# Undivided probabilities and transposed weights as the stationary operand in a decoder layer's prompt attentions

## The chip, the cores and the metric

The kernel runs on one core of a Trainium2 chip. The metric is the device time of one execution in microseconds. Three runs of the kernel before gave 4417.42, 4426.75 and 4428.59 us; the median is 4426.75 us. One more execution was profiled, and every row below is from that one.

Five engines run side by side, each strictly in the order of its own instruction list: TensorE (PE, whose weight loads are listed apart as PEld), VectorE (DVE), ScalarE (ACT), GpSimd (POOL) and SyncE (SP, which only starts transfers).

## The reference, cut to what matters

One layer of a hybrid decoder is computed for a prompt of 1024 tokens and for 64 sample tokens. Two of its parts are touched here, for the prompt only: the FoX attention (8 heads of 64, causal, with a forgetting term added to the scores) and the attention over 256 memory tokens (4 heads of 128). Both end in the same two steps, a softmax and a product with the values:

```python
# FoX, block by block of 128 queries
s = einsum('bqhd,bkhd->bhqk', qi, k) * scale + (di - dk)
s = where(k_pos <= pi, s, -inf)
p = softmax(s, axis=-1)
o = einsum('bhqk,bkhd->bqhd', p, v)
# memory
p = softmax(einsum('bthd,bmhd->bhtm', q, mk) * MEM_HD ** -0.5, axis=-1)
o = einsum('bhtm,bmhd->bthd', p, mv)
```

The division of the softmax is by one sum for each query and head, so it can be made on the probabilities or on the output. Around this lie a gated linear attention (GLA), three output projections with gates, and PEER: each token picks 128 of 16384 experts and sums what they give.

## The kernel before, in words

The tokens are cut into nine blocks: prompt blocks 0 to 7 of 128 tokens, and the sample block. `base(grp)` takes three groups in turn: [0, 1, 2], [3, 4, 5] and [sample, 6, 7]. For a group it runs all projections, GLA, FoX, memory attention, gates, output projection and the scores of PEER. Queries and heads are worked in two halves: half 0 has FoX heads 0 to 3 and memory heads 0 and 1, half 1 the others. So `fox_prompt` and `mem_prompt_att` are each called 16 times, once for a block and half.

The experts of blocks 0, 1, 2, 6 and 7 are gathered row by row (`peer_gather`): POOL starts an indirect transfer of 512 KB (L1040 for u, L1051 for v), and DVE works on the 128 x 1024 tile that landed (L1042 for u, L1057 for v). That is 256 such tiles for a block, with four buffers. Blocks 0 to 2 are gathered beside the base work of groups 1 and 2; blocks 6 and 7 beside the dense stage. The other four blocks go through `peer_dense`, which multiplies all experts on PE and ends the kernel.

The order is set by the tile framework: it takes the instructions in program order, moves the gather to a later priority, and lets a simulated timeline choose for each engine which ready instruction comes next. [...]

In `fox_prompt` the keys come in chunks of up to 512 columns: one chunk for blocks 0 to 3, two for blocks 4 to 7. For each head PE makes the scores in a PSUM bank `f` (two banks, L562, L563, L566), DVE takes the negated row maximum (L567, and L570 where there are two chunks), ACT makes the exponentials and their row sum (L575), DVE adds the sums (L578) and inverts (L579), ACT multiplies the probabilities by that (L581), PE transposes them into a bank `g` (two banks, L584), ACT copies them out (`PT`, by the helper `evac`, L99), and PE multiplies them with the values into `po` (one bank, L589). There the value columns of a head (64) are the stationary operand and the transposed probabilities (128 columns) the moving one, so `po` holds the output transposed: head dimension on the partitions. One copy (L99, `oT<-po`) ends the call, and SP writes `oT` to memory (L659). `mem_prompt_att` does the same for two heads at once (L598, L601, L604, L605, L607, L610, L99, L616).

float32 matmuls stand in the trace as two records each (L589: 576 records for 288 matmuls); a transpose is one record.

## Time and profile before

| | us |
|---|---|
| median of three runs | 4426.75 |
| the profiled execution, as a whole | 4433.77 |
| its span, first to last instruction | 4432.0 |
| base work of group 0, no gather beside it | 0 to some 710 |
| base work of groups 1 and 2, gather of blocks 0 to 2 beside it | some 710 to 2690 |
| end of group 2, start of the dense stage | 2690 to some 3100 |
| dense stage | 3108 to 4432 |

The FoX calls stand at 235 to 278 and 360 to 403 us (group 0, half 0 and half 1), 938 to 1029 and 1152 to 1244 us (group 1), 1968 to 2048 and 2214 to 2303 us (group 2). The memory calls stand at 400 to 436, 1249 to 1285 and some 2608 to 2632 us.

A table of stretches lists for each engine the busy time in it and, in brackets, the number of instructions, then the granted TensorE clock (PEclk, share of full speed), the busy share of the DMA engines and what they moved. A group of instructions has its busy time, the mean of one in ns, and the idle time of its engine just before them with what ended it.

### The profile page before, as it was taken

To read this page: it belongs to the slowest core of one execution; us is meant where nothing else is said; L and a number is where in the kernel's file an instruction comes from. 1 tells how busy PE (TensorE), PEld (TensorE's weight loads), DVE (VectorE), ACT (ScalarE), POOL (GpSimd) and SP (SyncE) were. 2 spreads that over 40 slices of the span, in tenths; PEclk is the share of its full clock that TensorE was granted. 3 is DMA by queue.
4 is the path that set the end of the run, shared out by engine and by line. 5 is a ranking of instruction groups with operands and counts; after the bars stand their busy time and mean duration, and the time that the engine had idled before them with its cause. 6 is when DMAs were issued, how large, how long until landed. Compare 5 with 4: busy or idle time off the path is not lost. (4 is left out here: it accounts for less than half of the span.)

```text
span 4432.0 us, 62344 instructions
## 1 busy us (share of the span) xinstructions
PE 3755.6 (85%) x21306; PEld 3288.8 (74%) x21306; DVE 3346.1 (75%) x7924; ACT 1796.2 (41%) x3637; POOL 1679.1 (38%) x1466
## 2 busy tenths in 40 slices
PE   4998998676689775787679979986999999999998
PEld 4886997564378775575556558875999899999997
DVE  3443469988788898888885457578999888888883
ACT  2555444343343333465564334444333223323332
POOL 0000003545644444534455553003445454545530
PEclk8997998787689886677689989997999999999999
DMA  3322457888899987778788899548999999999982
GB/s 110 90 84 70 131 165 227 279 274 294 277 309 332 319 267 242 260 243 273 253 277 287 307 321 320 169 140 289 329 303 339 327 332 337 341 337 327 344 297 81
DMA packets 652340, 1141.32 MB, mean 258 GB/s; under 512 B 62158, under 2 KB 445798, under 8 KB 648439
## 3 DMA queue, kind: packets, MB, share of 16 engines
q0 software_dynamic: 193616, 704.99, 45.6%
q1 hardware_dynamic: 458406, 432.35, 30.3%
q8 instruction: 169, 2.77, 0.2%
q14 instruction: 149, 1.21, 0.1%
HBM read 1073.45 MB, written 63.74 MB: 257 GB/s over the span
## 5 line engine op out<-in xcount | busy, mean ns | idle before, releaser
L1040 POOL DMA_INDIRECT u<-in_peer_u_dram,ei x640 | 783.3, 1224 | 873.2 <-DVE a L1042 347.6
L1051 POOL DMA_INDIRECT v<-in_peer_v_dram,ei x640 | 762.3, 1191 | 865.0 <-DVE acc L1057 452.6
L1042 DVE CUSTOM_DVE_ANT_0 u<-u,x 128x1024 f32<-128x1024 f32 x640 | 774.2, 1219 | 129.9 <-DMA u<-in_peer_u_dram,ei 128.3
L1057 DVE SCALAR_TENSOR_TENSOR acc<-v,a,acc 128x1024 f32<-128x1024 f32 x635 | 811.6, 1278 | 70.6 <-DMA v<-in_peer_v_dram,ei 68.2
L265 ACT ACTIVATE wh<-wr 128x512 fp32r<-128x512 f32 x568 | 354.0, 630 | 595.0 <-PE pj L274 186.2
L267 DVE TENSOR_TENSOR wl<-wr,wh 128x512 fp32r<-128x512 f32 x568 | 386.6, 685 | 219.4 <-PE pj L277 63.8
L1210 PE MATMUL py<-dwh,dvh 128*128 128x448 f32 x1024 | 373.9, 370 | 31.3 <-ACT dwh L1197 28.6
L1187 PE MATMUL pa<-xh,duh 128*128 128x448 f32 x1024 | 384.8, 376 | 1.3 <-ACT duh L1168 1.3
L1188 PE MATMUL pa<-xl,duh 128*128 128x448 f32 x1024 | 379.0, 370 | 0.0
L273 PE MATMUL pj<-aT,wh 128*128 128x384 f32 (+1 forms) x1104 | 367.3, 337 | 11.4 <-ACT X L837 4.5
L1211 PE MATMUL py<-dwl,dvh 128*128 128x448 f32 x1024 | 375.4, 367 | 1.4 <-DVE dwl L1198 1.4
L1212 PE MATMUL py<-dwh,dvl 128*128 128x448 f32 x1024 | 373.4, 368 | 0.3 <-DVE dvl L1206 0.3
L274 PE MATMUL pj<-aT,wh 128*128 128x384 f32 (+1 forms) x1104 | 362.3, 332 | 1.7 <-DVE aT L317 1.7
L281 PE MATMUL pj<-wh,aT 128*128 128x256 f32 x944 | 262.1, 301 | 30.3 <-DVE z L720 10.9
L1205 ACT ACTIVATE dvh<-dvr 128x1024 fp32r<-128x1024 f32 x128 | 134.2, 1059 | 377.2 <-PE py L1211 206.6
L282 PE MATMUL pj<-wh,aT 128*128 128x256 f32 x944 | 258.8, 297 | 2.9 <-DVE aT L847 1.5
L277 PE MATMUL pj<-aT,wl 128*128 128x384 f32 (+1 forms) x1104 | 251.8, 335 | 10.3 <-DVE wl L267 10.1
L1117 PE MATMUL cw<-hot,hot 128*128 128x128 f32 x768 | 173.9, 363 | 92.7 <-ACT stg L1118 73.8
L1190 PE MATMUL pa<-xh,dul 128*128 128x448 f32 x1024 | 240.2, 369 | 0.0
L1117 PEld LDWEIGHTS cw<-hot,hot 128*128 128x128 f32 x768 | 134.8, 248 | 138.1 <-ACT stg L1118 103.3
L1210 PEld LDWEIGHTS py<-dwh,dvh 128*128 128x128 f32 x1024 | 192.4, 189 | 48.6 <-ACT dwh L1197 28.9
L273 PEld LDWEIGHTS pj<-aT,wh 128*128 128x128 f32 x1104 | 213.1, 193 | 17.4 <-ACT X L837 6.6
(475 smaller groups left out, 8439.3 us busy)
## 6 DMA issues: line engine op xcount, KB each, us to landing
wr<-in_w_in_dram SPq DMA_DIRECT2D x168, 512.0 KB, 4.8
dvr<-in_peer_v_dram SPq DMA_DIRECT2D x128, 512.0 KB, 7.5
dur<-in_peer_u_dram SPq DMA_DIRECT2D x128, 512.0 KB, 6.6
dc<-c_scr SPq DMA_DIRECT2D x15, 1792.0 KB, 17.4
wr<-in_w_pq_dram SPq DMA_DIRECT2D x48, 512.0 KB, 4.3
c_scr<-stg SPq DMA_DIRECT2D x24, 1024.0 KB, 6.9
wr<-in_w_out_dram SPq DMA_DIRECT2D x24, 512.0 KB, 4.8
u<-in_peer_u_dram,ei POOLq DMA_INDIRECT x640, 6.2
```

Of the source, the lines that this page charges most:

```text
L267: V.tensor_tensor(wl, raw[:, q2:q2 + 2], wh.bitcast(F32), op=OP.subtract)
L273: PE.matmul(ps, wh[:, i, c], hi[:, k], start=k == 0, stop=False)
L274: PE.matmul(ps, wh[:, i, c], lo[:, k], start=False, stop=False)
L1040: G.indirect_dma_start(out=r, out_offset=None, in_=UR, in_offset=bass.IndirectOffsetOnAxis(ap=ei[:, s:s + 1], axis=0))
L1042: V.tensor_tensor_reduce(r, r, x2, 1.0, 0.0, OP.mult, OP.add, a[:, s:s + 1])
L1051: G.indirect_dma_start(out=r, out_offset=None, in_=VR, in_offset=bass.IndirectOffsetOnAxis(ap=ei[:, s:s + 1], axis=0))
L1057: V.scalar_tensor_tensor(acc, r, a[:, s:s + 1], acc, op0=OP.mult, op1=OP.add)
L1187: PE.matmul(pa[:, :NT], uh[:, k], xh[:, k], start=k == 0, stop=False)
L1188: PE.matmul(pa[:, :NT], uh[:, k], xl[:, k], start=False, stop=False)
L1210: PE.matmul(py[:, :NT], vh[:, j], wh, start=j == 0, stop=False)
L1211: PE.matmul(py[:, :NT], vh[:, j], wl, start=False, stop=False)
L1212: PE.matmul(py[:, :NT], vl[:, j], wh, start=False, stop=j == DG - 1)
```

## The change

The multiplication of the probabilities by the inverted sum (L581, L607) is taken out. The transposed probabilities become the stationary operand and the values the moving one, so `po` holds the output with the queries on the partitions, the four heads of a half side by side. There, once in a call, DVE adds the sums of all four heads, inverts them, and multiplies `po` by them into a tile `o` (from the pool `ge`, three buffers). Two PE transposes into a `g` bank and a copy then give `oT` as before.

```diff
         po = PS("po")
+        l = T("sm", [128, 8])
...
-                l = T("sm", [128, 4])
...
-                    A.activation(pm[:, :n], ps[ci][:, :n], AF.Exp, bias=nm[:, 0:1], accum_out=l[:, ci:ci + 1])
...
-                if len(chunks) == 2:
-                    V.tensor_tensor(l[:, 0:1], l[:, 0:1], l[:, 1:2], op=OP.add)
-                V.reciprocal(l[:, 2:3], l[:, 0:1])
...
-                    A.activation(Pm[ci][:, :n], Pm[ci][:, :n], AF.Copy, scale=l[:, 2:3])
...
+                A.activation(pm[:, :n], ps[ci][:, :n], AF.Exp, bias=nm[:, 0:1], accum_out=l[:, 4 * ci + hh:4 * ci + hh + 1])
...
-                        PE.matmul(po[64 * e:64 * e + 64, j * 128:(j + 1) * 128],
-                                  vv[:, kb, (2 * j + e) * 64:(2 * j + e + 1) * 64],
-                                  pts[:, i * 128:(i + 1) * 128], start=kb == 0, stop=kb == blk)
-        evac(oT, po[:, :256].rearrange("p (j t) -> p j t", t=128))
+                    PE.matmul(po[:, hh * 64:(hh + 1) * 64], pts[:, i * 128:(i + 1) * 128],
+                              vv[:, kb, hh * 64:(hh + 1) * 64], start=kb == 0, stop=kb == blk)
+        if nc_ == 2:
+            V.tensor_tensor(l[:, 0:4], l[:, 0:4], l[:, 4:8], op=OP.add)
+        V.reciprocal(l[:, 0:4], l[:, 0:4])
+        o = T("ge", [128, 256])
+        V.tensor_tensor(o.rearrange("p (h d) -> p h d", h=4), po[:, :256].rearrange("p (h d) -> p h d", h=4),
+                        l[:, 0:4, None].to_broadcast([128, 4, 64]), op=OP.mult)
+        pt = PS("g")
         for j in range(2):
+            PE.transpose(pt[:, j * 128:(j + 1) * 128], o[:, j * 128:(j + 1) * 128], ident)
+        evac(oT, pt[:, :256].rearrange("p (j t) -> p j t", t=128))
```

`mem_prompt_att` is changed in the same way (L607 goes, the operands of L616 change places, and a multiplication, two transposes and the copy follow).

Because the lists are chosen anew, all of them move a little. Below, rows of the lists are shown without times; names are tiles with their buffer numbers, and lines are those of the kernel that the list belongs to. In the changed kernel the scores are L565, L566 and L569, the maximum L570, the transposes L579, the value product L584, the multiplication L590 and the last transposes L594; the gather's u and v instructions are L1050 and L1065.

PE, group 1, half 0, from the last transposes of block 4's fourth head on; in the kernel before:

```order
L584 MATMUL g_11119<-c_76,P_11112 128x128 x4
L584 MATMUL g_11131<-c_76,P_11114 128x128
L589 MATMUL po_10991<-PT_11124,kv_10339 64x128 x4
L589 MATMUL po_10991<-PT_11133,kv_10339 64x128
L562 MATMUL f_11179<-c_270,c_196 128x512
L563 MATMUL f_11179<-kv_10338,zq_10895 128x512
L562 MATMUL f_11183<-c_270,c_196 128x256
```

The same place in the changed kernel:

```order
L569 MATMUL f_11117<-c_88,c_78 128x128
L584 MATMUL po_10974<-kv_10327,PT_11087 128x64 x4
L584 MATMUL po_10974<-kv_10327,PT_11097 128x64
L594 MATMUL g_11104<-c_76,ge_11102 128x128 x2
L579 MATMUL g_11125<-c_76,P_11123 128x128 x4
L565 MATMUL f_11146<-c_270,c_196 128x512
L566 MATMUL f_11146<-kv_10326,zq_10883 128x512
```

The last transposes of a block (L594) now stand straight behind its last value product, and the next head's transposes and scores behind them.

DVE, the same place (the first two heads of block 5); in the kernel before:

```order
L567 TENSOR_REDUCE sm_11140<-f_11141 128x1
L567 TENSOR_REDUCE sm_11140<-f_11145 128x1
L570 TENSOR_TENSOR sm_11140<-sm_11140 128x1
L1042 ISA u_7425,a_7055<-u_7425,x_1341_7053 128x1024
L1042 ISA a_7055 128x1
L578 TENSOR_TENSOR sm_11151<-sm_11151 128x1
L579 RECIPROCAL sm_11151<-sm_11151 128x1
L1042 ISA u_7428,a_7055<-u_7428,x_1341_7053 128x1024
L1042 ISA a_7055 128x1
L567 TENSOR_REDUCE sm_11178<-f_11179 128x1
L567 TENSOR_REDUCE sm_11178<-f_11183 128x1
```

In the changed kernel (L588 inverts the sums of block 4, L590 multiplies its output):

```order
L588 RECIPROCAL sm_10975<-sm_10975 128x4
L267 TENSOR_TENSOR wl_12264<-wr_12244,wh_12262 128x512
L570 TENSOR_REDUCE sm_11112<-f_11113 128x1
L1050 ISA u_7407,a_7043<-u_7407,x_1347_7041 128x1024
L1050 ISA a_7043 128x1
L570 TENSOR_REDUCE sm_11112<-f_11117 128x1
L1050 ISA u_7410,a_7043<-u_7410,x_1347_7041 128x1024
L1050 ISA a_7043 128x1
L590 TENSOR_TENSOR ge_11102<-po_10974,sm_10975 128x256
L573 TENSOR_TENSOR sm_11112<-sm_11112 128x1
L1050 ISA u_7413,a_7043<-u_7413,x_1347_7041 128x1024
L1050 ISA a_7043 128x1
```

The adding and inverting for each head is gone from between the maxima; the multiplication stands once, behind a gather tile.

DVE, group 2, where the third output projection is gated (the two L842, L850 in the changed kernel, of its second quarter of columns); in the kernel before:

```order
L1057 SCALAR_TENSOR_TENSOR acc_8912<-v_9592,a_8809,acc_8912 128x1024
L267 TENSOR_TENSOR wl_24304<-wr_24300,wh_24302 128x512
L1016 TENSOR_TENSOR acc_8912<-acc_8912,h_9595 128x1024
L841 TENSOR_TENSOR X_24290<-f_24254,X_24290 128x320
L841 TENSOR_TENSOR X_24294<-f_24255,X_24294 128x320
L267 TENSOR_TENSOR wl_24320<-wr_24300,wh_24318 128x512
L267 TENSOR_TENSOR wl_24338<-wr_24334,wh_24336 128x512
L842 TENSOR_TENSOR z_23478<-z_23478,X_24290 128x320
L842 TENSOR_TENSOR z_23478<-z_23478,X_24294 128x320
```

In the changed kernel:

```order
L1065 SCALAR_TENSOR_TENSOR acc_8900<-v_9550,a_8797,acc_8900 128x1024
L267 TENSOR_TENSOR wl_24188<-wr_24168,wh_24186 128x512
L267 TENSOR_TENSOR wl_24216<-wr_24212,wh_24214 128x512
L1065 SCALAR_TENSOR_TENSOR acc_8900<-v_9553,a_8797,acc_8900 128x1024
L849 TENSOR_TENSOR X_24202<-f_24166,X_24202 128x320
L849 TENSOR_TENSOR X_24206<-f_24167,X_24206 128x320
L267 TENSOR_TENSOR wl_24232<-wr_24212,wh_24230 128x512
L850 TENSOR_TENSOR z_23390<-z_23390,X_24202 128x320
L267 TENSOR_TENSOR wl_24250<-wr_24246,wh_24248 128x512
L850 TENSOR_TENSOR z_23390<-z_23390,X_24206 128x320
```

Before, all 768 gather tiles of blocks 0 to 2 stand ahead of this place (L1016 is already the end of block 2); in the changed kernel 759 do, and nine follow it. At the start of group 2's first FoX call the lag is already eight tiles (493 and 485 ahead of it).

## Rows read from the trace of the kernel before

**Rows 1.** The page's first part: busy time, share of the span, instructions.

```profile
span 4432.0 us, 62344 instructions
...
PE 3755.6 (85%) x21306; PEld 3288.8 (74%) x21306; DVE 3346.1 (75%) x7924; ACT 1796.2 (41%) x3637; POOL 1679.1 (38%) x1466
```

**Rows 2.** Table of stretches, columns as in its header row: the six FoX stretches, two memory stretches, the stretch of the gather beside base work, its end, the dense stage.

```profile
core 0: us, PE busy (x) PEld busy (x) DVE busy (x) ACT busy (x) POOL busy (x), PEclk, DMA share, GB/s
235.00:278.00 43.00, 41.78 (x275) 32.87 (x273) 14.76 (x42) 33.05 (x77) 0.88 (x2) 0.96 0.25 71
360.00:403.00 43.00, 42.60 (x168) 27.03 (x168) 11.33 (x35) 22.44 (x69) 0.88 (x2) 0.68 0.13 40
400.00:436.00 36.00, 32.43 (x184) 29.29 (x183) 11.19 (x21) 26.42 (x66) 0.00 (x0) 0.91 0.43 140
938.00:1029.00 91.00, 79.21 (x485) 59.58 (x485) 72.84 (x159) 53.33 (x117) 46.43 (x39) 0.94 0.83 276
1152.00:1244.00 92.00, 74.34 (x298) 48.40 (x298) 68.41 (x120) 40.29 (x94) 56.71 (x45) 0.72 0.81 264
1249.00:1285.00 36.00, 28.84 (x146) 24.67 (x145) 25.89 (x34) 24.50 (x59) 14.45 (x15) 0.81 0.96 330
1968.00:2048.00 80.00, 72.03 (x411) 54.41 (x410) 68.07 (x208) 51.86 (x124) 31.38 (x30) 0.87 0.75 249
2214.00:2303.00 89.00, 71.18 (x342) 48.70 (x342) 75.45 (x154) 63.07 (x152) 50.90 (x41) 0.85 0.83 278
714.00:2690.00 1976.00, 1502.47 (x8453) 1207.62 (x8451) 1584.29 (x4056) 879.22 (x1919) 993.87 (x861) 0.81 0.84 285
2690.00:2775.00 85.00, 81.86 (x539) 81.30 (x540) 68.18 (x96) 39.65 (x72) 23.32 (x20) 0.96 0.88 299
3108.00:4432.00 1324.00, 1295.66 (x6778) 1189.00 (x6776) 1109.08 (x1763) 405.55 (x642) 595.02 (x485) 0.99 0.89 307
```

**Rows 3.** What ended DVE's idle time in 1152 to 1244 us (releaser, us, times, longest).

```profile
DVE u L1042 <- DMA u<-in_peer_u_dram,ei: 9.5, 11, 1.5
DVE acc L1057 <- DMA v<-in_peer_v_dram,ei: 7.2, 6, 3.2
DVE sm L567 <- PE f L563: 2.6, 2, 1.9
DVE sm L567 <- PE f L566: 2.2, 2, 1.2
DVE sm L579 <- ACT P L575: 0.9, 2, 0.7
DVE sm L578 <- ACT P L575: 0.9, 1, 0.9
```

**Rows 4.** Groups of instructions over the whole span, what the change removes: busy, mean ns of one, idle before and its releaser.

```profile
L581 ACT ACTIVATE P<-P,sm 128x512 f32<-128x512 f32 x48 | 33.6, 715 | 40.9 <-DVE sm L579 36.2 <-DVE ch L983 4.5
L607 ACT ACTIVATE P<-P,sm 128x256 f32<-128x256 f32 x32 | 14.2, 509 | 1.9 <-DVE sm L605 1.9
L579 DVE RECIPROCAL sm<-sm 128x1 f32<-128x1 f32 x64 | 10.0, 156 | 10.9 <-ACT P L575 10.7
L578 DVE TENSOR_TENSOR sm<-sm x32: 130/154/200, 964.5 to 2294.3; 128x1 f32<-128x1 f32 x32
```

**Rows 5.** Groups that bound what it adds: a DVE operation of 128x256 with one operand in PSUM, the gather's two DVE operations, and two of PE.

```profile
L863 DVE TENSOR_TENSOR z<-pj,ge 128x256 f32<-128x256 f32 x33 | 12.3, 417 | 10.6 <-PE pj L285 7.4 <-DMA ge<-in_x_prompt_dram 3.2
L1042 DVE CUSTOM_DVE_ANT_0 u<-u,x 128x1024 f32<-128x1024 f32 x640 | 774.2, 1219 | 129.9 <-DMA u<-in_peer_u_dram,ei 128.3
L1057 DVE SCALAR_TENSOR_TENSOR acc<-v,a,acc 128x1024 f32<-128x1024 f32 x635 | 811.6, 1278 | 70.6 <-DMA v<-in_peer_v_dram,ei 68.2
L589 PE MATMUL po<-PT,kv 128*64 128x128 f32 x576 | 91.4, 312 | 5.9 <-ACT PT L99 5.9
```

**Rows 6.** Timeline: start us, us for the run of records, engine, line, operands, partitions*columns of the stationary operand, moving operand, records. Eight transposes; eight value products with 128 stationary and 128 moving columns (memory); eight matmuls with 128 stationary and 64 moving columns; eight value products of FoX.

```profile
405.41 1.04 PE L610 MATMUL g<-c,P 128*128 128x128 f32 x8
409.08 1.05 PE L616 MATMUL po<-PT,pg 128*128 128x128 f32 x8
2301.09 1.09 PE L1248 MATMUL g<-c,kv 64*128 64x64 f32 x8
2302.11 1.09 PE L589 MATMUL po<-PT,kv 128*64 128x128 f32 x8
```

**Rows 7.** Groups on PE: the waits for the multiplied probabilities, FoX and memory.

```profile
L584 PE MATMUL g<-c,P 128*128 128x128 f32 x288 | 57.2, 337 | 19.4 <-ACT P L581 19.2
L610 PE MATMUL g<-c,P 128*128 128x128 f32 x64 | 14.1, 352 | 9.2 <-ACT P L607 9.2
```

**Rows 8.** Timeline at the end of a memory call and the start of the next one's value product.

```profile
2612.80 2.08 PE L616 MATMUL po<-PT,pg 128*128 128x128 f32 x8
...
2614.91 0.38 ACT L99 ACTIVATE oT<-po 128x256 f32<-128x256 f32 x1 [1.31 <-PE po L616]
...
2615.35 1.75 PE L616 MATMUL po<-PT,pg 128*128 128x128 f32 x8 [0.47 <-ACT oT L99]
```

More of the change, by code (lines that the diff above doesn't have):

```diff
@@ L552, in fox_prompt @@
         chunks = [(c, min(512, nk - c)) for c in range(0, nk, 512)]
+        nc_ = len(chunks)
         po = PS("po")
[L554 to L591 removed]
@@ L592, in fox_prompt @@
-        evac(oT, po[:, :256].rearrange("p (j t) -> p j t", t=128))
+        l = T("sm", [128, 8])
+        for hh in range(4):
+            j, e = hh // 2, hh % 2
+            h = 4 * half + hh
+            R = slice(64 * e, 64 * e + 64)
+            ps, nm = [], T("sm", [128, 4])
+            for ci, (c, n) in enumerate(chunks):
+                p = PS("f")
+                diag = c + n == nk
+                PE.matmul(p[:, :n], selr[:, h, :].to_broadcast([128, 128]), nd[:, c:c + n], start=True, stop=False)
+                PE.matmul(p[:, :n], qT[R, j, :], kT[R, j, c:c + n],
+                          start=False, stop=not diag)
+                if diag:
+                    PE.matmul(p[:, n - 128:n], identb, caus, start=False, stop=True)
+                V.tensor_reduce(nm[:, ci:ci + 1], p[:, :n], axis=AX.X, op=OP.max, negate=True)
+                ps.append(p)
+            if nc_ == 2:
+                V.tensor_tensor(nm[:, 0:1], nm[:, 0:1], nm[:, 1:2], op=OP.min)
+            for ci, (c, n) in enumerate(chunks):
+                pm = T("P", [128, 512])
+                A.activation(pm[:, :n], ps[ci][:, :n], AF.Exp, bias=nm[:, 0:1], accum_out=l[:, 4 * ci + hh:4 * ci + hh + 1])
+                pt = PS("g")
+                for i in range(n // 128):
+                    PE.transpose(pt[:, i * 128:(i + 1) * 128], pm[:, i * 128:(i + 1) * 128], ident)
+                pts = T("PT", [128, 512])
+                evac(pts[:, :n], pt[:, :n])
+                for i in range(n // 128):
+                    kb = c // 128 + i
+                    PE.matmul(po[:, hh * 64:(hh + 1) * 64], pts[:, i * 128:(i + 1) * 128],
+                              vv[:, kb, hh * 64:(hh + 1) * 64], start=kb == 0, stop=kb == blk)
@@ L605, in mem_prompt_att @@
         V.reciprocal(l, l)
-        for i in range(2):
-            A.activation(pm[:, i, :], pm[:, i, :], AF.Copy, scale=l[:, i:i + 1])
         pt = PS("g")
@@ L615, in mem_prompt_att @@
             for b in range(2):
-                PE.matmul(po[:, i * 128:(i + 1) * 128], mv[:, b, i * 128:(i + 1) * 128], pts[:, 2 * i + b, :],
+                PE.matmul(po[:, i * 128:(i + 1) * 128], pts[:, 2 * i + b, :], mv[:, b, i * 128:(i + 1) * 128],
                           start=b == 0, stop=b == 1)
-        evac(oT, po[:, :256].rearrange("p (j t) -> p j t", t=128))
+        o = T("ge", [128, 256])
+        V.tensor_tensor(o.rearrange("p (h d) -> p h d", h=2), po[:, :256].rearrange("p (h d) -> p h d", h=2),
+                        l[:, :, None].to_broadcast([128, 2, 128]), op=OP.mult)
+        pt = PS("g")
+        for j in range(2):
+            PE.transpose(pt[:, j * 128:(j + 1) * 128], o[:, j * 128:(j + 1) * 128], ident)
+        evac(oT, pt[:, :256].rearrange("p (j t) -> p j t", t=128))
     h_scr = [dp.tile([128, 1024], F32, name=f"h_scr{b}") for b in range(9)]
```

30 lines of the change are left out of this document (2 added, 28 removed).

## The prediction

> **What bounds the kernel now.** I read the page's totals first, then the table of stretches, then in the stretches that the change touches what ended the idle time of DVE, and last the single groups and a few pieces of the timeline.
>
> The totals [rows 1] put PE first (85% busy), DVE next (75%), ACT far behind (41%). They are an average over stages with different limits, so the stretches decide [rows 2]. [...] The FoX calls of group 0 (235 to 278 and 360 to 403 us) have PE busy 41.78 and 42.60 of 43 us and DVE busy a third of the time or less: PE and the loop through it set the pace. [...] In the FoX calls of groups 1 and 2 (91 + 92 + 80 + 89 = 352 us) the picture is another: DVE is busy 72.84 + 68.41 + 68.07 + 75.45 = 284.8 us, 81%, PE 84% at clocks of 0.72 to 0.94. What DVE has there is mostly gather. And its idle time ends mostly on the gather's transfers: 16.7 us in the second stretch, against 4.8 on PE's scores and 1.8 on ACT's exponentials [rows 3]. So the attention's own chain decides only part of these stretches; it is what the change shortens.
>
> **What goes.** ACT loses 96 multiplications in FoX, of which the 48 of 512 columns are 33.6 us, and 14.2 us in the memory attention [rows 4]; with the narrower 48 forms (between the 509 ns of 256 columns and 715 ns, estimated at some 0.5 us each, 24 us) some 72 us of ACT's time in all. ACT is 41% busy, so this is worth nothing by itself. It counts where somebody waits for it: PE idled 19.2 us for the multiplied probabilities in FoX and 9.2 us in memory [rows 7], 28.4 us. Those transposes will wait for the exponential instead. That ends earlier by the inversion (0.156 us) and the multiplication (0.5 to 0.7 us) plus DVE's queue: ACT itself idled 36.2 us for the inversion, since it sits behind gather tiles of 1.2 us [rows 4, 5]. Some of the saved wait meets the next one, the maximum of the next head. Ends: nothing to 28.4 us; I take half, **-14 us**.
>
> DVE loses 64 inversions of 0.156 us (10.0 us) and 32 additions of 0.154 (4.9 us) [rows 4]. It gains 16 inversions (2.6 us) and 8 additions (1.2 us) at those prices and 32 multiplications of 128x256 out of PSUM. The nearest row is L863, the same shape, one operand in PSUM: 417 ns [rows 5], 13.4 us. That is 17.2 for 14.9 us: DVE's work as a whole stays (+2.3 us, hidden in its idle fifth). What goes is 10.7 us [rows 4] of waiting for a sum before an inversion, and the like before the additions. In group 0 this hides under PE. In groups 1 and 2 I take **-5 us** (0 to 9).
>
> **What comes on PE.** The value product keeps its 352 matmuls, and so its records. Before, a FoX record has 64 columns loaded and 128 moved; now 128 loaded and 64 moved. Eight such records in a row take 1.09 us before (L589), eight with 128 loaded and 64 moved (L1248) also take 1.09 us, eight with 128 and 128 take 1.05 us [rows 6]. A 128-column load costs as much as a 128-column pass: **0 us**. The bounds of this are -30 us (half the 0.11 us of 576 records) and +5 us.
>
> [...]
>
> The last transposes are 64 records of 0.11 us (L610: eight in 1.04 us, the last one's run included) [rows 6]: 7.0 us, of which the 24 of group 0 stand where PE is full: **+2.7 us**. In groups 1 and 2, PE has the idle time to hide them.
>
> **The new wait.** The multiplication needs the last value product, and the last transposes need the multiplication. On PE's list I counted how much stands between the last value product and those transposes: in 14 of the 32 calls two rows or fewer, five of them in group 0. There PE stands still, and with it the next head's scores and the projections behind. The trace has such a step in the memory calls, with a copy in place of the multiplication: value product to 2614.88, copy of 0.38 us, next value product at 2615.35, PE idle 0.47 us [rows 8]. With 0.42 us for 0.38 that is 0.5 us. In group 0 DVE is free: 5 x 0.5 = **+2.5 us**. In groups 1 and 2 a gather tile of 1.22 to 1.28 us may be running on DVE: 0.5 to 1.8 us each, for nine calls 4.5 to 16; I take 1.1 each, 10 us, and half of it on the path, because PE is not what ends these stretches: **+5 us**. In the other 18 calls PE has work between. SP's start of `oT` is later by multiplication and transposes, under 1 us plus queues; weight transfers stand behind it but are loaded four tiles ahead: 0.
>
> **What moves.** The new lists put the gather later against the base work: eight tiles at group 2's first FoX call, nine at the third output projection's gate. There before, the gather was through. So DVE does nine tiles less up to there, 9 x 1.25 = 11.3 us, and does them from about 2690 us on, where DVE has 16.8 us idle in 85 and PE is busy 81.86 [rows 2]: hidden. DVE is 80% busy until then (1584.29 of 1976 us, same rows), so I take four fifths: **-9 us** (0 to -11).
>
> **Sum.** -14 - 5 + 0 + 2.7 + 2.5 + 5 - 9 = -17.8 us. On the profiled execution (4433.77 us, its span 4432.0 and 1.8 around it) that gives 4416; this execution lies 7.0 us above the median of the runs shown, 4426.75, so the forecast against them is **4409 us**, 0.4% faster. Its own range, with the terms' bounds taken half, is 4392 to 4422.
>
> **Rivals.**
>
> *Nothing to see.* DVE's work doesn't shrink (17.2 for 14.9 us), and its idle time in the FoX stretches of groups 1 and 2 ends mostly on gather transfers, which move 249 to 278 GB/s there whatever the attention does. Then a shorter chain only means a longer wait for the next tile: the terms of 14 and 9 us fall to a few, and the 10 us added eat them: 4419 to 4435. For it: rows 3. Against it: ACT's 36 us of waiting stood between DVE and the weight conversions that feed PE.
>
> *Slower: the multiplication behind the gather.* Place: the end of each of the 20 calls in groups 1 and 2, where the multiplication stands on DVE's list behind one gather tile or more, and the only `po` bank and PE's list wait for it. At 1.8 us each this is 36 us on the path instead of 5; if also half of the gains stay, the sum is 36 + 5.2 - 14 = +27, 4454; at one and a half tiles in only ten of the calls, +15 or so. It decides as soon as most of these calls stand still for a whole tile. For it: DVE is 81% busy there, and the list shows the multiplication behind a tile. Against it: PE has slack of its own there, and a block's first value product comes a head later than its scores.
>
> *Much faster.* All waits tied to the multiplied probabilities go: 28.4 us of PE's and 36.2 us of ACT's, with some 10 us of new ones: -55, 4372. Against it: the two overlap, and a third of the calls are in group 0, where PE is full.
>
> *Half the value product.* If 64 moving columns halve the records after all, up to 30 us of PE's time go, of which the part in group 0 and where PE leads counts: with the other terms some -35, 4392. Against it: L1248.
>
> **How the numbers follow.** The chances: forecast 0.45, nothing to see 0.22, slower 0.16, much faster 0.12, half the value product 0.05. Some 0.3%, 13 us, is what a measurement of this kernel can tell from no change (the three runs lie 11 us apart), so faster ends at 4413.5 and slower begins at 4440. The forecast's own range reaches across 4413.5 with a quarter of its chance: 0.34 faster and 0.11 the same. Faster: 0.34 + 0.12 + 0.05 + 0.01 = 0.52; the same: 0.11 + 0.20 and a little of the slower case, 0.32; slower 0.16. The range for 8 in 10 goes from 4385 to 4442: it leaves out the much faster case and half of the slower one, 0.2 together.
>
> **What would show it.** In the profile after: ACT's busy time lower by some 72 us, DVE's within 5 us, PE's the same or a little above. No idle time of PE for a multiplied probability; in its place the transposes wait for the exponentials, less than 15 us in all. The value product's eight records still in some 1.05 to 1.1 us. A multiplication of 0.42 us, 32 times, and a wait of PE for it of 0.5 us in group 0's memory calls. The FoX stretches of groups 1 and 2 shorter by 2 to 6 us each, those of group 0 not. The dense stage equally long and 15 to 20 us earlier. I am wrong if the dense stage itself changes its length, if PE's waits for the multiplication pass 15 us, or if the base of groups 1 and 2 takes as long as before although ACT waits less.

## The result and the profile after

The changed kernel takes 4457.57 us (median of six runs, 4445.64 to 4465.01) where the kernel before takes 4425.43 beside it: a ratio of 1.0078, 95% interval 1.0058 to 1.0097. It is 32 us slower; the forecast was 18 us faster, with a range that ended at 4442.

The profiled execution (4465.01 us) is read in the order of the prediction. First the totals, which answer to [rows 1]:

```profile
span 4463.1 us, 62327 instructions
...
PE 3805.6 (85%) x21370; PEld 3336.8 (75%) x21370; DVE 3347.6 (75%) x7884; ACT 1730.6 (39%) x3505; POOL 1667.9 (37%) x1466
```

ACT has lost 65.6 us, where some 72 were expected, and DVE's work is the same within 1.5 us, as expected. PE has 64 records more, and 50 us more of busy time: 64 transposes at 0.11 us don't make that.

The table of stretches, with the columns of [rows 2], cut at the first and last FoX records of the late calls and at the gather and dense stages:

```profile
core 0: us, PE busy (x) PEld busy (x) DVE busy (x) ACT busy (x) POOL busy (x), PEclk, DMA share, GB/s
...
957.00:1063.00 106.00, 99.11 (x541) 77.64 (x540) 86.65 (x165) 49.84 (x109) 53.99 (x48) 0.81 0.90 305
1170.00:1269.00 99.00, 85.31 (x287) 59.43 (x288) 70.01 (x106) 28.57 (x71) 56.94 (x49) 0.53 0.79 260
1956.00:2056.00 100.00, 86.13 (x483) 65.58 (x481) 81.68 (x243) 53.60 (x121) 39.76 (x37) 0.84 0.77 250
2222.00:2314.00 92.00, 81.77 (x310) 56.64 (x310) 68.48 (x122) 45.39 (x115) 48.43 (x40) 0.61 0.74 242
722.00:2713.00 1991.00, 1548.03 (x8502) 1246.50 (x8501) 1576.32 (x4032) 830.65 (x1825) 986.88 (x850) 0.78 0.83 280
3130.00:4463.00 1333.00, 1299.17 (x6781) 1190.79 (x6779) 1105.86 (x1758) 403.38 (x643) 578.06 (x486) 0.99 0.88 306
```

The reader is to look at the second and the fourth row, half 1 of groups 1 and 2: the granted clock is 0.53 and 0.61 of full speed, where [rows 2] had 0.72 and 0.85. The clock has two levels here: its records in both traces hold 0.50 and 1.00 and nothing between (70 spells at each before, 54 after), and the figure of a stretch is their mean. After, the whole of 1107 to 1263 us reads 0.50. PE is busy 85 us of 99 there with *fewer* records (287 against 298): each lasts longer. The four FoX stretches of before and after aren't cut alike (352 us with 1536 PE records, 397 us with 1621), so their lengths alone don't say where the time went.

The groups show the same. First the scores and the forgetting term before, then all four groups of FoX after:

```profile
L563 PE MATMUL f<-kv,zq 64*128 64x512 f32 (+3 forms) x192 | 100.3, 608 | 0.0
...
L562 PE MATMUL f<-c,c 128*128 128x512 f32 (+3 forms) x96 | 44.9, 473 | 20.8 <-ACT P L575 20.7
```

```profile
L566 PE MATMUL f<-kv,zq 64*128 64x512 f32 (+3 forms) x192 | 123.9, 739 | 0.5 <-ACT zq L793 0.5
...
L584 PE MATMUL po<-kv,PT 128*128 128x64 f32 x576 | 101.5, 340 | 0.8 <-ACT PT L99 0.8
...
L579 PE MATMUL g<-c,P 128*128 128x128 f32 x288 | 67.7, 362 | 18.8 <-ACT P L576 18.8
...
L565 PE MATMUL f<-c,c 128*128 128x512 f32 (+3 forms) x96 | 52.6, 554 | 10.7 <-ACT P L576 10.1 <-ACT kv L99 0.5
```

The scores aren't touched by the change, have the same shapes and the same count, and cost 23.6 us more. With the value product (+10.1 against [rows 5]), the transposes (+10.5 against [rows 7]) and the forgetting term (+7.7) that is 51.9 us, as much as PE's busy time grew in all (50.0). The new last transposes (L594 and L625) add 8.2 + 8.1 = 16.3 us, and other groups together gave back some 18. A piece of the timeline of after, half 1 of group 1 (columns as in [rows 6]), shows one head:

```profile
1199.36 1.11 PE L579 MATMUL g<-c,P 128*128 128x128 f32 x4 [1.36 <-ACT P L576]
1200.12 0.77 PE L565 MATMUL f<-c,c 128*128 128x512 f32 x1
1200.83 2.07 PE L566 MATMUL f<-kv,zq 64*128 64x512 f32 x2
```

and the same two groups of before, in the same call:

```profile
1186.74 0.49 PE L562 MATMUL f<-c,c 128*128 128x512 f32 x1
1187.17 1.12 PE L563 MATMUL f<-kv,zq 64*128 64x512 f32 x2
```

The two score records of 512 columns take 2.07 us at a clock of 0.50, for 1.12 at 1.00. Last, PE's waits in both attentions (releaser, us, times, longest):

```profile
PE g L579 <- ACT P L576: 18.8, 13, 3.1
...
PE g L625 <- DVE ge L621: 11.6, 8, 2.9
PE f L565 <- ACT P L576: 10.1, 3, 4.5
PE po L617 <- ACT PT L99: 9.5, 8, 3.0
...
PE g L594 <- DVE ge L590: 8.5, 5, 4.1
...
PE g L611 <- ACT P L607: 5.4, 4, 2.8
```

The waits for the new multiplication are 8.5 + 11.6 = 20.1 us; the waits for the probabilities, 28.4 before [rows 7], are 18.8 + 5.4 = 24.2. The scores waited 20.7 us for an exponential before (L562) and wait 10.1 after (L565). The dense stage starts late (its first matmul at 2988.4 us for 2962.5), and its own length, 1333 for 1324 us, explains little: from the first matmul of its first line (L1187 before, L1195 after) to the last of that line it takes 1407.1 for 1402.1 us, and 1391.6 to 1408.9 in the kernels below that don't touch it either.

So three theories. **Clock**: the value product now moves 64 columns a record, and with such records TensorE's granted clock falls to the lower level, 0.50, in FoX. **Wait**: the stops for the multiplication at the end of each call. **Chain** or **lists**: the order came out otherwise, and that alone costs.

### The profile page after: what moved, and what is told of

The parts are those of the page before. It is cut to its first block, busy times and chain, and to the rows that moved or that the text cites. A ratio compares the mean times of both kernels' runs of the same rounds, so it can differ in the third digit from the quotient of the medians.

```text
span 4463.1 us, 62327 instructions
## 1 busy us (share of the span) xinstructions
PE 3805.6 (85%) x21370; PEld 3336.8 (75%) x21370; DVE 3347.6 (75%) x7884; ACT 1730.6 (39%) x3505; POOL 1667.9 (37%) x1466
## 5 line engine op out<-in xcount | busy, mean ns | idle before, releaser
L1050 DVE CUSTOM_DVE_ANT_0 u<-u,x 128x1024 f32<-128x1024 f32 x640 | 774.2, 1222 | 119.4 <-DMA u<-in_peer_u_dram,ei 118.1
L1065 DVE SCALAR_TENSOR_TENSOR acc<-v,a,acc 128x1024 f32<-128x1024 f32 x635 | 813.8, 1282 | 65.6 <-DMA v<-in_peer_v_dram,ei 61.8
L1195 PE MATMUL pa<-xh,duh 128*128 128x448 f32 x1024 | 384.0, 375 | 2.1 <-ACT duh L1176 2.1
L281 PE MATMUL pj<-wh,aT 128*128 128x256 f32 x944 | 257.4, 297 | 23.3 <-DVE z L728 6.3
L1125 PE MATMUL cw<-hot,hot 128*128 128x128 f32 x768 | 182.9, 377 | 97.3 <-ACT stg L1126 79.7
L282 PE MATMUL pj<-wh,aT 128*128 128x256 f32 x944 | 253.3, 292 | 1.8 <-DVE aT L317 1.3
```

The source lines that it names most:

```text
L1050: V.tensor_tensor_reduce(r, r, x2, 1.0, 0.0, OP.mult, OP.add, a[:, s:s + 1])
L1065: V.scalar_tensor_tensor(acc, r, a[:, s:s + 1], acc, op0=OP.mult, op1=OP.add)
L1195: PE.matmul(pa[:, :NT], uh[:, k], xh[:, k], start=k == 0, stop=False)
```

## The experiments

The table gives, for each whole kernel, its median, its ratio to the kernel before on the same chip (interval in brackets), the granted clock in 1140 to 1260 and in 2200 to 2320 us (both late FoX calls with what is around them), and the mean of one score record. In e1 and e4 the output is left undivided.

| run | us | ratio | clock | clock | scores, ns |
|---|---|---|---|---|---|
| before | 4425.43 | 1 | 0.74 | 0.79 | 608 |
| changed | 4457.57 | 1.0078 [1.0058, 1.0097] | 0.50 | 0.60 | 739 |
| e1_old_sides | 4430.44 | 1.0021 [1.0006, 1.0036] | 0.69 | 0.77 | 660 |
| e2_swap_only | 4446.26 | 1.0044 [1.0022, 1.0066] | 0.50 | 0.72 | 706 |
| e3_wide | 4428.03 | 1.0004 [0.9992, 1.0016] | 0.63 | 0.74 | 672 |
| e4_no_mult | 4436.61 | 1.0031 [1.0016, 1.0046] | 0.56 | 0.64 | 714 |
| e5_mem_only | 4440.17 | 1.0020 [1.0003, 1.0037] | 0.66 | 0.78 | 639 |
| e6_fox_only | 4452.82 | 1.0060 [1.0038, 1.0082] | 0.53 | 0.69 | 700 |
| e7_wide_act | 4420.47 | 0.9989 [0.9970, 1.0008] | 0.72 | 0.76 | 675 |
| e8_before_fill | 4433.05 | 1.0011 [0.9996, 1.0026] | 0.72 | 0.81 | 612 |
| e9_after_fill | 4466.91 | 1.0100 [1.0075, 1.0124] | 0.59 | 0.60 | 686 |
| e10_fox_wide_act | 4420.90 | 0.9990 [0.9976, 1.0005] | 0.64 | 0.74 | 680 |
| e11_neutral | 4421.98 | 0.9999 [0.9983, 1.0014] | 0.81 | 0.84 | 601 |
| e12_swap_wide | 4435.76 | 1.0032 [1.0013, 1.0050] | 0.70 | 0.75 | 642 |
| n1_after_neutral | 4434.25 | 1.0013 [0.9996, 1.0030] | 0.53 | 0.57 | 702 |
| n2_wide_neutral | 4438.43 | 1.0021 [1.0006, 1.0035] | 0.67 | 0.73 | 669 |
| n3_after_neutral2 | 4447.80 | 1.0044 [1.0027, 1.0062] | 0.50 | 0.61 | 727 |
| n4_wide_act_neutral | 4411.39 | 0.9939 [0.9917, 0.9961] | 0.70 | 0.82 | 662 |

### One part undone at a time

**e1_old_sides**, the values stationary again:

```diff
-                    PE.matmul(po[:, hh * 64:(hh + 1) * 64], pts[:, i * 128:(i + 1) * 128],
-                              vv[:, kb, hh * 64:(hh + 1) * 64], start=kb == 0, stop=kb == blk)
+                    PE.matmul(po[64 * e:64 * e + 64, j * 128:(j + 1) * 128],
+                              vv[:, kb, hh * 64:(hh + 1) * 64],
+                              pts[:, i * 128:(i + 1) * 128], start=kb == 0, stop=kb == blk)
...
-        V.reciprocal(l[:, 0:4], l[:, 0:4])
...
+        evac(oT, po[:, :256].rearrange("p (j t) -> p j t", t=128))
```

> Undivided probabilities as in the changed kernel, but the values are the stationary operand again, no last transposes, one copy ends a call; the division by the sums is left out altogether (sums and inversions of FoX too), so the output is undivided. [...] Theory 'chain' (with the multiplication on ScalarE gone, PE does its FoX work in other pieces or another order, and that alone costs): 4445 or more, and the clock stays at 0.5 to 0.6 there.

27 us of the 32 are gone, and the clock is back to 0.69 (the clock theory expected 0.70 or more). That speaks against the chain, but doesn't part clock from wait, since both expected the loss to be gone, at 4400 to 4425 us. Both missed in part: the time is 5 us above that range, and the scores take 660 ns, not the 608 of before. With neither multiplication nor division nor last transposes the kernel still isn't faster than before. PE's waits for the exponentials there:

```profile
PE g L579 <- ACT P L576: 42.6, 17, 7.9
...
PE f L565 <- ACT P L576: 4.0, 2, 3.3
```

At the same two places the kernel before waited 19.2 us for the multiplied probabilities [rows 7] and 20.7 for the exponentials: 39.9 us, for 46.6 here. Taking work off the chain bought waiting.

**e2_swap_only**, the swap without the rest (in memory the same way):

```diff
-                        PE.matmul(po[64 * e:64 * e + 64, j * 128:(j + 1) * 128],
-                                  vv[:, kb, (2 * j + e) * 64:(2 * j + e + 1) * 64],
-                                  pts[:, i * 128:(i + 1) * 128], start=kb == 0, stop=kb == blk)
+                        hh = 2 * j + e
+                        PE.matmul(po[:, hh * 64:(hh + 1) * 64], pts[:, i * 128:(i + 1) * 128],
+                                  vv[:, kb, hh * 64:(hh + 1) * 64], start=kb == 0, stop=kb == blk)
+        o = T("ge", [128, 256])
+        A.activation(o, po[:, :256], AF.Copy)
```

> The kernel before, with the divided probabilities kept (multiplications on ScalarE), only the sides of both value products swapped; a ScalarE copy of the output and two transposes end a call. Theory 'clock': slower than before by 20 to 45 us (4445 to 4470), the granted clock in the FoX stretches of groups 1 and 2 at 0.5 to 0.65. Theory 'wait': no multiplication of VectorE at the end, the copy takes its place: 4425 to 4440, clocks as before. Theory 'chain': 4425 to 4433, clocks as before.

Slower by 20 us at a clock of 0.50, with every multiplication of the probabilities still in place: the swap does it, together with the copy and the last transposes that it needs (e12 below has those too). In the last calls the clock fell less than expected (0.72).

**e3_wide**, 128 value columns moved:

```diff
-                    PE.matmul(po[:, hh * 64:(hh + 1) * 64], pts[:, i * 128:(i + 1) * 128],
-                              vv[:, kb, hh * 64:(hh + 1) * 64], start=kb == 0, stop=kb == blk)
+                    PE.matmul(po[:, hh * 128:(hh + 1) * 128], pts[:, i * 128:(i + 1) * 128],
+                              vv[:, kb, j * 128:(j + 1) * 128], start=kb == 0, stop=kb == blk)
```

> The changed kernel, but in FoX each record moves 128 value columns (both heads of a pair) into its own 128 columns of the output bank, of which the multiplication reads the 64 that count; it does so in two instructions of half the size. The number of records is the same. Theory 'clock': the records are as long as before, the granted clock in FoX goes back to 0.70 to 0.85, and 20 to 35 us come back: 4420 to 4438. Theories 'wait' and 'chain': no change, 4450 to 4462 (the second multiplication adds up to 0.2 us a call).

29 us come back, although PE moves twice the columns in the product and half of what it makes is thrown away. The clock rises as the theory said, to 0.74 in the last calls; the 0.63 of the first window lies below its range.

**e4_no_mult**, nothing of VectorE at the end of a call:

```diff
-        V.reciprocal(l[:, 0:4], l[:, 0:4])
...
+        A.activation(o, po[:, :256], AF.Copy)
```

> The changed kernel, but the output is copied by ScalarE instead of being multiplied by VectorE, and the sums and inversions of FoX are left out, so the output is undivided in both attentions. Nothing at the end of a call waits for VectorE's list. Theory 'wait': 25 to 35 us come back, 4420 to 4435. Theory 'clock': 4445 to 4458, FoX clocks as in the changed kernel. Theory 'chain': 4445 to 4458 as well.

Between the two: 21 us come back, though the clock stays low. PE's wait at this place is 5.9 us there in memory, now for ScalarE, and under 2 us in FoX. So the wait may have a part; n1 below gains as much with the multiplication in place.

**e5_mem_only** and **e6_fox_only** take one of the two changed functions each (e6's edit is the FoX part of the change; e5's core is this):

```diff
-                PE.matmul(po[:, i * 128:(i + 1) * 128], mv[:, b, i * 128:(i + 1) * 128], pts[:, 2 * i + b, :],
+                PE.matmul(po[:, i * 128:(i + 1) * 128], pts[:, 2 * i + b, :], mv[:, b, i * 128:(i + 1) * 128],
```

> The kernel before with the changed memory attention alone (FoX as before). Theory 'clock' (64 moving columns a record in FoX lower the granted clock there): the memory product keeps 128 columns on either side, so the loss isn't here; what is left is its wait for the multiplication (11.6 us of TensorE's idle time in the changed kernel) less the waits it saves (9.2): 4420 to 4435. Theory 'wait' (the stops at the end of a call are the loss): 4435 to 4445.

> The kernel before with the changed FoX attention alone (memory as before). Theory 'clock': nearly the whole loss is here, 4445 to 4460, with a granted clock of 0.5 to 0.6 between 1140 and 1260 us. Theory 'wait': half of the loss, since FoX has 8.5 of the 20.1 us of waits for a multiplication, 4435 to 4445, clocks wherever they fall.

FoX has most of the loss and most of the fall in the clock; the memory attention, with 128 columns on either side, costs 9 us by its ratio, at clocks of 0.66 and 0.78, and came out 5 us above the clock theory's range, inside that of the wait.

**e12_swap_wide** puts wide records into e2:

```diff
-                                  vv[:, kb, hh * 64:(hh + 1) * 64], start=kb == 0, stop=kb == blk)
+                                  vv[:, kb, j * 128:(j + 1) * 128], start=kb == 0, stop=kb == blk)
```

> The swap alone (divided probabilities, copy by ScalarE, two last transposes) with 128 value columns moved in FoX. Theory 'clock': of the 20 us that the swap alone cost, 10 to 20 come back, 4425 to 4436, with FoX clocks of 0.65 to 0.80. Otherwise 4446 as without.

The clock rises from 0.50 to 0.70 in the first window, and the ratio falls only from 1.0044 to 1.0032, some 5 us: within the theory's times, but by itself no proof, since the intervals overlap. That most of e2's 20 us come from the width isn't shown.

### How much the lists alone move

**e11_neutral**, **n1_after_neutral**, **n2_wide_neutral** (and n3 with a second such line):

```diff
                 ps, nm = [], T("sm", [128, 4])
+                V.memset(nm[:, 3:4], 0.0)
```

> The kernel before with 64 more instructions on VectorE that do nothing for the result (a fill of 128x1, one a head, ahead of the scores), as a control for how much the time moves when only the lists fall out otherwise. They are some 0.06 us each, 4 us of VectorE's time, not on the path: 4423 to 4432 if the lists don't matter; 4435 or more, or 4415 or less, if lists alone move the time by as much as the runs that lie within 10 us of the kernel before.

> The changed kernel with the control's 64 fills of 128x1 on VectorE. Theory 'clock': 4447 to 4467, as the changed kernel. If the changed kernel's 4457 is how its lists happened to fall out: 4420 to 4440.

> The wide run with the same fills. Theory 'clock': 4420 to 4436, as the wide run. If the wide run's 4428 is how its lists happened to fall out: 4445 or more.

> The changed kernel with two such fills a head, which shifts its lists once more. Theory 'clock': 4447 to 4467. Lists: 4420 to 4440.

The kernel before stays (4422 us, 1 us below the range for lists that don't matter). The 0.06 us of a fill is an estimate: in the trace of before a 128x1 inversion starts at 236.63 us and VectorE's next instruction at 236.69. The changed one takes 4457, 4434 and 4448 us with three sets of lists, the wide one 4428 and 4438: n1 and n2 both miss the clock theory's range (n3 is inside it), and their lists alone are worth 10 to 23 us. Part of what the lists move is the wait for the multiplication: 20.1 us in the changed kernel, 11.7 in n1 and 10.1 in n3. So a single pair of kernels doesn't settle a difference of this size here. Taken together they do better. The seven kernels with 64 moving columns in FoX (changed, e2, e4, e6, e9, n1, n3) have ratios of 1.0013 to 1.0100, mean 1.0053; the other ten variants 0.9939 to 1.0032, mean 1.0003: some 0.5%, 22 us, between the means, with overlap. In the clocks there is none: in both windows each of the seven lies below each of the others and below before (0.50 to 0.59 against 0.63 to 0.81, and 0.57 to 0.72 against 0.73 to 0.84), and so with the scores' mean (686 ns and more against 680 and less).

The same column shows a second thing. Where the product's records are as wide as before or wider, the scores take 601 to 642 ns with divided probabilities (before, e5, e8, e11, e12) and 660 to 680 with undivided ones (e1, e3, e7, e10, n2, n4). So taking the multiplication out goes with longer records too, by about as much as the narrow records add.

### The call by itself

**m1_calls_alone**:

```diff
+    for nb in (0, 2):
+        nbusy[0] = nb
+        for f in (fox_b, fox_a, fox_w, fox_u):
+            tc.strict_bb_all_engine_barrier()
+            for rep in range(3):
+                o = T("oT", [128, 2, 128])
+                f(7, 0, qTm_[:, :, :128], kTm, vvm, o)
```

> The kernel before with measured pieces ahead of it: the FoX call of block 7, three times in a row each, in four forms (as before; as changed; changed with wide records; undivided with the values stationary), with a barrier of all engines between the forms, no gather and no projections beside it; then the four forms again with two multiplications of 128x1024 on VectorE (about 1.2 us each, estimated from the gather's tiles) ahead of each head's maximum, as the gather puts them there. The inputs of these calls are rows of the prompt, and their results are used by nothing. Theory 'clock': in one or both passes the changed form shows a granted clock lower by 0.1 or more than the form before and the wide form, and its three calls take 5 us or more longer than the wide ones. Otherwise (lists): the four forms' clocks lie within 0.05, and the changed form is the shortest or the same, as its chain is shorter.

The table of stretches of this run, one row a form (before, changed, wide, undivided with the values stationary; then the four again with VectorE's extra work):

```profile
56.17:139.90 83.73, 79.70 (x372) 45.93 (x372) 22.41 (x60) 45.38 (x98) 0.00 (x0) 1.00 0.00 1
140.42:267.33 126.91, 124.60 (x378) 78.87 (x378) 20.82 (x45) 32.25 (x74) 0.00 (x0) 0.52 0.00 1
267.85:347.86 80.01, 77.45 (x378) 47.36 (x378) 21.01 (x48) 32.26 (x74) 0.00 (x0) 0.90 0.00 1
348.38:429.97 81.59, 77.40 (x372) 46.35 (x372) 18.52 (x36) 32.26 (x74) 0.00 (x0) 0.90 0.00 1
430.49:515.49 85.00, 77.41 (x372) 45.05 (x372) 48.79 (x84) 46.17 (x98) 0.00 (x0) 0.94 0.00 1
516.01:643.93 127.92, 124.61 (x378) 78.86 (x378) 48.31 (x69) 32.26 (x74) 0.00 (x0) 0.52 0.00 1
644.45:728.88 84.43, 78.28 (x378) 47.95 (x378) 48.36 (x72) 32.04 (x74) 0.00 (x0) 0.89 0.00 1
729.40:816.05 86.65, 78.68 (x372) 47.40 (x372) 46.17 (x60) 32.26 (x74) 0.00 (x0) 0.88 0.00 1
```

This settles the mechanism for the call by itself. Three calls, in one execution, take 126.91 us in the changed form, 83.73 in the form before, 80.01 in the wide one: 14 to 16 us a call, far more than expected. Nothing else runs there, and PE is busy 124.60 of 126.91 us, so waits have hardly a part. PE's groups in the changed form's first stretch,

```profile
L667 PE MATMUL f<-kv,zq 64*128 64x512 f32 x48 | 47.8, 1097 | 0.0
L685 PE MATMUL po<-kv,PT 128*128 128x64 f32 x192 | 43.3, 420 | 0.0
L680 PE MATMUL g<-c,P 128*128 128x128 f32 x96 | 25.8, 426 | 1.8 <-ACT P L677 1.8
```

and in the wide form's:

```profile
L716 PE MATMUL f<-kv,zq 64*128 64x512 f32 x48 | 30.7, 724 | 0.0
L734 PE MATMUL po<-kv,PT 128*128 128x128 f32 x192 | 25.3, 287 | 0.1
L729 PE MATMUL g<-c,P 128*128 128x128 f32 x96 | 16.3, 295 | 1.8 <-ACT P L726 1.8
```

The records of all three groups are longer by 44 to 52%, the untouched scores too. When the clock changes is seen in the timeline. Two score records take 1.12 us at the upper level and 2.07 at the lower one. In the changed form:

```profile
142.34 1.12 PE L667 MATMUL f<-kv,zq 64*128 64x512 f32 x2
...
145.41 1.11 PE L680 MATMUL g<-c,P 128*128 128x128 f32 x4 [1.79 <-ACT P L677]
...
150.36 2.07 PE L667 MATMUL f<-kv,zq 64*128 64x512 f32 x2
...
152.44 3.62 PE L685 MATMUL po<-kv,PT 128*128 128x64 f32 x16
```

and in the wide form, which begins at the lower level:

```profile
280.33 2.07 PE L716 MATMUL f<-kv,zq 64*128 64x512 f32 x2
...
282.42 3.07 PE L734 MATMUL po<-kv,PT 128*128 128x128 f32 x16
...
286.09 1.12 PE L716 MATMUL f<-kv,zq 64*128 64x512 f32 x2
```

In the changed form the clock falls in the gap of 1.79 us, some 8 us before the first value product: the score records ahead of it take 1.12 us a pair, and four transposes behind it 1.11 us, where [rows 6] had eight in 1.04. So it isn't the narrow records that lower it here. Each of the eight forms has a piece at the lower level near its start, also the first, where the clock column reads 1.00 but the score records take 2.07 us a pair up to 69 us. What differs is the rise: the wide form is back at the upper level some 17 us after its start, while its first value products run, and the last form after 18 us; the changed form isn't back in the 120 us that are left of it, in either pass. PE is busy 98% of the changed form's stretch (124.60 of 126.91 us), and the clock stays down.

The whole kernel looks the same in half 1 of group 1. In steps of 10 us, both kernels stand at or near 0.50 from 1110 to 1150 us; then the kernel before rises, to 1.00 by 1230, and the changed one stays at 0.50 until 1260. Why a stream with narrow records doesn't rise isn't shown.

The last form, without the multiplication and at the same price for a product, is 0.7 us a call shorter than the form before in the first pass, where both have some 17 us at the lower level. In the second pass it is 0.5 us longer, at 0.88 for 0.94. More than that the removed work isn't worth here.

### Filling, and the division elsewhere

**e8_before_fill** and **e9_after_fill** put one matmul ahead of each group of transposes:

```diff
                 pt = PS("g")
+                PE.matmul(pt[:, :n], selr[:, h, :].to_broadcast([128, 128]), nd[:, c:c + n], start=True, stop=True)
```

> The kernel before, with one more matmul of as many columns as the scores have put ahead of each group of FoX transposes, into the bank that these then overwrite: 96 records that compute nothing, and that TensorE makes while it would wait for the probabilities. Theory 'clock' (what TensorE moves in these stretches sets its granted clock): the clock in the FoX stretches of groups 1 and 2 rises to 0.85 or more, and the scores there are shorter; the time stays or falls, 4400 to 4428. If the clock follows something else: no higher clock, and 96 records of some 0.3 us more, of which half on the path: 4435 to 4450.

> The changed kernel (64 value columns a record) with the same filling as in the run on the kernel before: 96 records of up to 512 columns ahead of the FoX transposes, 36,864 columns in all, as many as the wide records add (576 x 64). If the clock follows how many columns TensorE moves in these stretches, wherever they come from: clock of 0.63 to 0.80 in the late FoX stretches and 4425 to 4440 us. If it is the product's own records that have to be wide: clock 0.50 to 0.60 and 4457 us or more, by the 96 records (up to +25).

On the kernel before the clock doesn't rise beyond what it was, and 4433 us misses both ranges by a little. On the changed one the time rises by 9 us, and with clocks of 0.59 and 0.60 that is what was expected if the product's own records have to be wide; the clock rises in the first window only. The four groups shown above fall from 345.7 to 322.5 us, and the 96 filling records cost 48.6 us themselves.

**m2_fills_alone** tries them in the calls alone, again in one execution (fox_f and fox_g with one and two fillings, fox_s the swap with divided probabilities, fox_h the form before with one):

```diff
+    for f in (fox_a, fox_f, fox_g, fox_s, fox_h):
+        tc.strict_bb_all_engine_barrier()
```

> The kernel before with five more forms of the block 7 call ahead of it, three calls each, by themselves: the changed one again; changed with the filling (24 matmuls of 512 columns ahead of the transposes); changed with twice that filling; the swap with divided probabilities; the form before with the filling. If columns moved anywhere hold the clock: the filled forms go back to 0.85 or more, and the singly filled one takes 85 to 100 us instead of 127, the price being its 24 matmuls of some 0.5 us. If only the product's own records count: it stays at 0.52, 140 us or more. The swap with divided probabilities, at the same narrow records: 0.5 to 0.6 and 125 us or more in the first case and the second. The form before with filling: 1.00 and 90 to 97 us.

```profile
56.18:185.61 129.43, 127.12 (x378) 79.46 (x378) 20.82 (x45) 32.23 (x74) 0.00 (x0) 1.00 0.00 0
186.13:271.71 85.58, 83.92 (x402) 52.74 (x402) 20.81 (x45) 32.12 (x74) 0.00 (x0) 1.00 0.00 1
272.23:357.47 85.24, 84.40 (x426) 54.04 (x426) 20.81 (x45) 32.13 (x74) 0.00 (x0) 0.95 0.00 1
357.99:450.91 92.92, 90.00 (x378) 54.75 (x378) 22.42 (x60) 46.94 (x101) 0.00 (x0) 0.76 0.00 1
451.43:540.34 88.91, 87.59 (x396) 50.21 (x396) 22.40 (x60) 45.37 (x98) 0.00 (x0) 0.90 0.00 1
```

In the first row and at the start of the second the clock column can't be right: the score records last 1138 ns in the first form, as in m1 at 0.52, and 724 in the second, as in m1 at 0.90. By the durations the first form stays at the lower level, and the second leaves it some 19 us after its start. With 24 useless matmuls more, the three calls take 85.58 us instead of 129.43. Value products of the same shape last

```profile
L632 PE MATMUL po<-kv,PT 128*128 128x64 f32 x192 | 43.3, 420 | 0.0
...
L681 PE MATMUL po<-kv,PT 128*128 128x64 f32 x192 | 26.0, 284 | 0.3 <-ACT PT L99 0.3
```

in the first form and in the second: at one level of the clock such a record costs what one with the sides of before does (285 ns in fox_h). So in the call alone it needn't be the product's own records that bring the clock back. Two misses: the swap with divided probabilities takes 92.92 us at 0.76, milder than either theory had it, and fox_h is shorter than expected, at 0.90 and not 1.00. The first of them says more: with the same narrow records, but divided probabilities, the clock does rise, 46 us after the form's start. The narrow records alone don't keep it down for good; the undivided probabilities have a part. Why the filling fails in the whole kernel stays open in part: its own 48.6 us are the larger share, but why the clock stays at 0.60 in the last calls isn't shown.

**e7_wide_act**, **e10_fox_wide_act** (memory as before) and **n4_wide_act_neutral** (with the control's line) leave the division to ScalarE, on wide records:

```diff
-        V.tensor_tensor(o.rearrange("p (h d) -> p h d", h=4), po[:, :256].rearrange("p (h d) -> p h d", h=4),
-                        l[:, 0:4, None].to_broadcast([128, 4, 64]), op=OP.mult)
+        for hh in range(4):
+            c = hh * 128 + (hh % 2) * 64
+            A.activation(o[:, hh * 64:(hh + 1) * 64], po[:, c:c + 64], AF.Copy, scale=l[:, hh:hh + 1])
```

> The changed kernel with 128 value columns moved in FoX as in the wide run, and with the division made by ScalarE, head by head (four copies of 64 columns, or two of 128, scaled by the inverted sum), in place of VectorE's one multiplication. The output is whole. If clock and wait are two separate losses, both go: 4405 to 4422, faster than before. If the wait only cost through the clock (TensorE stands, and then finds a low clock), little more is won than by the wide records: 4422 to 4435. If ScalarE's four copies with TensorE waiting for them are worse than one multiplication: above 4435.

> FoX with undivided probabilities, wide records and the division on ScalarE; the memory attention as in the kernel before. The output is whole. If the memory change alone costs what its own run showed (9 us): 4408 to 4416, faster than before. If these differences of some 10 us come from how the lists fall out and not from the memory change: 4418 to 4432.

> The wide form with the division on ScalarE (4420, ratio 0.9989 before) with the control's 64 fills on VectorE. If it is faster than the kernel before by itself: 4410 to 4424. If that was one fortunate set of lists: 4426 to 4440.

All three compute the whole result and are 37 to 46 us below the changed kernel; e7 and e10 can't be told from the kernel before, n4 is 0.6% faster than it (0.9917 to 0.9961). e7 and n4 lie in their first ranges, e10 in its second: with e7's memory change or without it the time is the same. That speaks for lists behind e5's 9 us, but doesn't show it, since e7 divides on ScalarE there and e5 on VectorE. PE's waits at the end of a call in n4:

```profile
PE g L627 <- ACT ge L624: 5.6, 10, 0.8
...
PE g L596 <- ACT ge L593: 2.4, 5, 0.8
```

8.0 us for 20.1: ScalarE has no gather in its list. n4 beats both kernels, but its twin e7 shows that some 20 us of that lie in its lists; two sets are too few to say what the form itself is worth.

## Why the prediction was wrong

The step that failed is the term for the value product: "A 128-column load costs as much as a 128-column pass: **0 us**." As to a record at one clock it holds (284 against 285 ns in m2). What it left out is that the sides of the product, together with the undivided probabilities, change the clock for everything beside it (0.52 for 0.90 in the call alone). The sum priced the product alone, with +5 us as its worst end; measured in PE's busy time are +10.1 us for the product and +41.8 for scores, transposes and forgetting term, which the sum held fixed. [rows 2] showed 0.68 in group 0 and 0.72 to 0.94 in groups 1 and 2, between the two levels of 0.50 and 1.00; the prediction took the clock as given, and no rival named it.

By terms:

- **-14 and -5**, the shorter chain: the gain didn't come. PE's waits for the probabilities fell by 4.2 us and the scores' waits for the exponentials by 10.6, but PE's own records grew by more. e1, which has the shorter chain and none of the new work, waits longer (46.6 us for 39.9) and isn't faster than before; a part of that is its clock (scores of 660 ns for 608). *Nothing to see* had the direction: a shorter chain only waits longer.
- **+2.5 and +5**, the new wait: right in place, short in size. PE waits 13 times for the multiplication, where 14 calls were counted, but 20.1 us, past the 15 at which the prediction called itself wrong. That the multiplication itself takes 0.42 us (418 and 422 ns) was right. How much of this ends on the path isn't settled: e4 takes it away and gains 21 us, but neutral lists alone move the changed kernel by as much.
- **-9**, the gather tiles that moved: they did move (DVE busy 1576.32 us in the stretch of groups 1 and 2, for 1584.29 [rows 2]), and the stretch still grew from 1976 to 1991 us.
- **+2.7**, the last transposes: sized too small. The 64 records take 16.3 us of PE, not 7.0; how much of it is on the path isn't measured.
- The rival *Slower: the multiplication behind the gather* had nearly the right time, 4454, by another mechanism: that is luck. *Half the value product* is excluded: no run shows records halved by 64 moving columns (284 ns for 285 with 128 in m2, and 420 in the form that stays at the lower level).

How much of the 32 us lasts is an estimate from few sets of lists. Three sets of the changed kernel average 1.0045, 20 us above the kernel before, and differ by up to 29 us among themselves; two sets of the wide one average 1.0013, 6 us above it. So some 14 us go with the narrow records, and some 12 of the 32 with how this one set of lists fell out. That the clock lies behind the 14 is shown for the call alone; for the whole kernel it rests on the clocks and the means of the seven and the ten.

## What to carry to other kernels

Before exchanging the two sides of a matmul, look at the granted clock of the stretch: here it already swung between its levels (0.72 and 0.85 in half 1 of groups 1 and 2), and the records that move fewer columns cost most in the matmuls beside them; the row of their own group shows only a part (10.1 of 51.9 us). The call alone, between barriers, shows in one run a mechanism that whole kernels with a 0.5% scatter of lists show only in sum; its size it doesn't show (14 us a call alone, 32 us for all 16 FoX calls here). And where a scheduler makes the lists, run each form with two or three harmless shifts before believing a difference of 10 or 20 us.

## What was not expected of the hardware

In the changed form by itself the clock falls in a gap of 1.79 us, before the first narrow record, and then stays down for 120 us with PE busy 98% (124.60 of 126.91 us). With useless matmuls it rises: the same three calls take 85.58 us with 24 matmuls more and 129.43 without. And wide records, half of whose results nobody reads, make three calls shorter than narrow ones do (80.01 for 126.91 us).
